# Start of a one-core decoder kernel: first products' squares and splits moved off GpSimd, first weights on ScalarE's queue, fixed split order

## The chip, the cores and the metric

The kernel runs on one core of one Trainium2 chip. The core's engines work side by side, each through its own instructions in order: TensorE (PE; weight loads are shown as PEld), VectorE (DVE), ScalarE (ACT), GpSimd (POOL) and SyncE (SP, which issues transfers). The metric is the device time of one execution in microseconds (us); lower is better.

## The reference, cut to what matters

A two-layer decoder trunk on 256 tokens of 2048 columns in float32. Layer A is gated linear attention, layer B sliding-window attention; each is followed by a squared-ReLU MLP of 8192 columns. The change lies in layer A's first lines:

```python
def rmsnorm(x, g):
    xf = x.astype(jnp.float32)
    y = xf * lax.rsqrt(jnp.mean(xf * xf, axis=-1, keepdims=True) + EPS)
    return (y * g.astype(jnp.float32)).astype(x.dtype)
...
    proj = h @ w_in                      # h = rmsnorm(x, norm_mix[0])
    q, k, v, r, glr = jnp.split(proj, [...], axis=-1)
    log_a = jax.nn.log_sigmoid((glr @ w_g2 + b_g).astype(f32)) / GLA_GATE_TAU
```

## The kernel before

Everything is kept transposed: model columns on the 128 partitions, the 256 tokens along the free dimension. A product over 2048 columns is made in four chunks of 512 (`kq`, or `c`), each of four tiles of 128 (`k`). Every operand is split into a leading half and a correction (float32r), and a product is three matmuls: weights' leading half x operand's leading half, weights' correction x operand's leading half, weights' leading half x operand's correction. A tile `k` of `gemm_sta` is 12 matmuls of 256 columns (4 groups of weight columns x 3), so the first product, `gemm_k(0)`, is 16 such tiles, 192 matmuls.

Three steps make the operands of a tile, and they bear the names used below:

- `split_w`: weights land in `ws`; ScalarE casts them to `wh` (L122), VectorE subtracts to `wl` (L123). The first product loads and splits by single tiles (`step=1`, 256 KB, 128x512); later ones load 1 MB and split by two tiles (128x1024). There are three `ws` buffers and four `wh`/`wl` pairs of two tiles each.
- `scaled`: x times the norm's gain: ScalarE makes the leading half `act` (L226), VectorE the correction (L227). It is 128x256 a tile.
- `load_x` (L271 on) loads a chunk of x in two transfers of 256 KB, calls `scaled` four times and has GpSimd add up x's squares: `ssx` and `sqx`, 128x1024 each (L281, L284, L285); `rstd_x` folds them to `ss` (L295, L296).

The row norm itself (`rstd_of`, `along`) is applied after the products: it is due some half chunks later (`later`, `tick`), and TensorE multiplies `ss` by ones for it after the first half of the next product's first chunk. Between the two products lies `glr`, 16 matmuls of 512 columns into `tp`. `load_gate` loads the gates' weights `wg` (512 KB) on GpSimd's queue and splits them on GpSimd (L334, L335).

A scheduler orders each engine's instructions by program order and priority: transfers and splits of weights come 60 places ahead (`WPRI`), one transfer of x has priority 0 (`XPRI`). All these transfers but `wg` and the gain `go` are issued by SyncE, at most eight in flight: each further one waits until an earlier one has landed.

Before x is there, TensorE runs 11 idle products of ones (`WARM`).

Of the kernel before, what the change touches and what calls it, by code (L numbers as in the profile page):

```python
# [8 lines left out]
F32 = mybir.dt.float32  # L9
# [3 lines left out]
ALU = mybir.AluOpType  # L13
# [25 lines left out]
XPRI = 0  # L39
# [10 lines left out]
def yoco_kernel(ctx: ExitStack, tc: tile.TileContext, x, norms, mlp_w1, mlp_w2, a_w_in, w_glr, w_gate, a_g_o, a_w_o,  # L50
# [18 lines left out]
    # work beside the large products: due so many half pieces of weights later, so that its operands are there  # L69
# [20 lines left out]
    # the norms' gains: a tile of 128 model columns to a column  # L90
    gT = const.tile([P, 5 * KT], F32, name="gT")
    with tc.high_priority(offset=WPRI):
        nc.sync.dma_start(out=gT, in_=norms)
    G_MIX0, G_MIX1, G_MLP0, G_MLP1, G_KV = (gT[:, KT * i:KT * (i + 1)] for i in range(5))
    # the tensor engine's clock rises once the array has been busy for a while: let it be, until x is there
# [9 lines left out]
    def split_w(parts, step=4):  # L105
# [3 lines left out]
        with tc.high_priority(offset=WPRI):  # L109
            for k in range(0, 4, step):  # L110
                ks = slice(k, k + step)
                o = 0
                for ap in parts:
                    n = ap.shape[1]
                    nc.sync.dma_start(out=ws[:, ks, o:o + n],
                                      in_=ap[k * P:(k + step) * P].rearrange("(k p) n -> p k n", p=P))
                    o += n
            n = min(step, 2)
            for k in range(0, 4, n):
                wh, wl = halves[k // 2]  # L120
                js, ks = slice(k % 2, k % 2 + n), slice(k, k + n)
                nc.scalar.copy(out=wh[:, js, :o], in_=ws[:, ks, :o])  # L122
                nc.vector.tensor_sub(out=wl[:, js, :o], in0=ws[:, ks, :o], in1=wh.bitcast(F32)[:, js, :o])  # L123
# [5 lines left out]
    def gemm_mov(src, act, evac, step=4):  # L129
        """out[tok, n] of 512 columns: activations stationary, weights moving. Returns a function of kq."""  # L130
# [23 lines left out]
    def gemm_sta(src, act, evac, widths=(P, P, P, P), step=4):  # L154
        """out^T[n, tok] of up to 512 columns: weights stationary, activations moving. Returns a function of kq."""
# [3 lines left out]
        def run(kq):  # L159
            if kq == 0:  # L160
                accs.extend(bank([P, 2, T], "acc") for _ in range((nf + 1) // 2))
            halves = split_w(src(kq), step)
# [20 lines left out]
    def gemm_wide(src, act, evac, last=False):  # L183
        """As gemm_sta; of each 128 columns the leading product and the sum of the corrections, [2, tok], apart. last:
        the columns end one after the other."""
# [32 lines left out]
    def new_act():  # L218
        """512 of a product's contraction, [128, 4, half of the mantissa, tokens], and the halves alone."""
# [3 lines left out]
    def scaled(act, kt, src, gcol):  # L223
        """Tile kt of an operand chunk: src (x^T, 128 columns of the model) * gain."""
        ah, al, _ = act
        nc.scalar.activation(out=ah[:, kt], in_=src, func=AF.Copy, scale=gcol)  # L226
        nc.vector.scalar_tensor_tensor(out=al[:, kt], in0=src, scalar=gcol, in1=ah.bitcast(F32)[:, kt], op0=ALU.mult,  # L227
                                       op1=ALU.subtract)

    def rsqrt(o, v, src, mul, n):  # L230
        """o = (src * mul + EPS) ** -0.5, [128, n]."""
# [6 lines left out]
    def add_ss(ss, xt, first):  # L238
        """ss += x^2 of two tiles of 128 model columns."""
# [7 lines left out]
    def rstd_of(r, ss):  # L247
        """1 / rms of every token: token on the partition."""
# [6 lines left out]
    def along(rb, r):  # L255
        """The same with the tokens along the free dim, on all partitions."""
# [14 lines left out]
    def load_x(c):  # L271
        """512 columns of the model: as an operand, and their squares' sums."""
        for k in range(0, 4, 2):
            r = c * C + k * P
            with tc.high_priority(offset=XPRI if (c, k) == (0, 2) else WPRI):
                nc.sync.dma_start(out=xt[c][:, k:k + 2], in_=x[r:r + 2 * P].rearrange("(k p) t -> p k t", p=P))
        act0.append(new_act())
        for kt in range(4):
            scaled(act0[c], kt, xt[c][:, kt], G_MIX0[:, c * 4 + kt:c * 4 + kt + 1])
        if c == 0:  # L280
            nc.gpsimd.tensor_mul(out=ssx, in0=xt[c], in1=xt[c])  # L281
        else:
            sq = actp.tile([P, 4, T], F32, name="sqx", tag="act")
            nc.gpsimd.tensor_mul(out=sq, in0=xt[c], in1=xt[c])  # L284
            nc.gpsimd.tensor_add(out=ssx, in0=ssx, in1=sq)  # L285

    ssx = actp.tile([P, 4, T], F32, name="ssx", tag="act")
# [4 lines left out]
    rb4, rbq4 = (a.rearrange("p (o t n) -> p o t n", o=1, t=NT).broadcast_to([P, 2, NT, P]) for a in (rb, rbq))  # L292

    def rstd_x():
        nc.gpsimd.tensor_add(out=ss, in0=ssx[:, :2], in1=ssx[:, 2:])  # L295
        nc.gpsimd.tensor_add(out=ss[:, 0], in0=ss[:, 0], in1=ss[:, 1])  # L296
# [4 lines left out]
    # ================= layer A: gated linear attention =================  # L301
# [4 lines left out]
    # sums over the tokens up to each one: upwards in the first tile, downwards in the second  # L306
# [5 lines left out]
    # of every block of 2s partitions, the half with the earlier tokens  # L312
# [13 lines left out]
    # the gates' product, exact in two passes: glr in quarters of the partitions, see glr()  # L326
# [4 lines left out]
    def load_gate():  # L331
        wg = g2.tile([P, 1024], F32, name="wg", tag="mlev")
        nc.gpsimd.dma_start(out=wg, in_=w_gate)
        nc.gpsimd.tensor_copy(out=wgh, in_=wg)  # L334
        nc.gpsimd.tensor_sub(out=wgl, in0=wg, in1=wgh.bitcast(F32))  # L335
# [555 lines left out]
```

## Time and profile before

| | us |
|---|---|
| Runs, median of 3 | 2107.68 |
| Runs, lowest and highest | 2105.56, 2120.28 |
| Profiled execution, span on the core | 2105.1 |
| TensorE busy in it | 2083.7 (99%) |
| First product's first and last matmul start | 6.17, 48.53 |

The page gives no separate time for the profiled execution; the run nearest to its span is the lowest, 0.5 us above it. The span starts with the first instruction on the core. Busy time of an engine is not progress alone: an instruction that waits inside for a port counts as busy, and so do matmuls at the lower of TensorE's two clocks.

### The profile page before, as it was taken

The page shows a single profiled execution, that of the slowest core. Times are in us where ns is not written, and L with a number is a line of the kernel's source. Part 1 is how long each engine was busy: PE and PEld are TensorE (multiplying, and loading weights), DVE is VectorE, ACT ScalarE, POOL GpSimd, SP SyncE. Part 2 cuts the span into 40 slices and gives each one's busy share as a digit, 9 for nine tenths or more (in the row PEclk, how much of TensorE's full clock was granted, in tenths as well). Part 3 has the DMA queues.
Part 4 walks back from the last instruction along what each step waited for, and adds up shares of the span by engine and source line. Part 5 has one row for each costly group of instructions (what it writes and reads, how often), then busy time and mean ns, then how long its engine had stood idle before and what let it go on. Part 6 is the DMA issues. An engine that isn't in the chain of part 4 may idle for free.

```text
span 2105.1 us, 30277 instructions
## 1 busy us (share of the span) xinstructions
PE 2083.7 (99%) x12290; PEld 1835.0 (87%) x12290; DVE 1282.4 (61%) x1523; ACT 989.4 (47%) x1314; POOL 419.0 (20%) x338
## 2 busy tenths in 40 slices
PE   7999999999999999999999999999999999999999
PEld 6998889988888888888888878988888888888888
DVE  7587444765555555555578576775555655555555
ACT  4645454444434434434455676444434434443442
POOL 6054111322003102201233143232102201200310
PEclk8999999999999999999999999999999999999999
DMA  6544555555565555555655533555556555556564
GB/s 217 178 142 148 174 179 180 180 183 187 192 197 183 198 183 182 198 194 185 196 187 177 184 122 121 179 176 187 198 185 195 182 198 184 188 190 198 182 209 131
DMA packets 195884, 381.40 MB, mean 181 GB/s; under 512 B 6577, under 2 KB 14785, under 8 KB 195745
## 3 DMA queue, kind: packets, MB, share of 16 engines
q1 hardware_dynamic: 195424, 378.60, 54.5%
q8 instruction: 96, 1.57, 0.3%
q0 software_dynamic: 320, 0.87, 0.2%
q14 instruction: 44, 0.35, 0.0%
HBM read 377.35 MB, written 2.10 MB: 180 GB/s over the span
## 4 chain that ended last, share of the span: by engine, by line
PE 93%; DVE 3%; ACT 2%; DMA 1%; issue 1%; POOL 1%; SPq 0%; ACTq 0%; DVEq 0%
PE acc L81 53%; PE ms L81 20%; PE tp L81 18%; DVE wl L123 1%; ACT sc L784 1%; DMA ws<-in_a_w_in_dram 1%; DVE act L227 0%; PE tp L717 0%; ACT wh L122 0%; POOL ss L245 0%; DMA xt<-in_x_dram 0%; DVE xt L584 0%; PE tp L530 0%; DVE st L778 0%; DVE st L780 0%
## 5 line engine op out<-in xcount | busy, mean ns | idle before, releaser
L123 DVE TENSOR_TENSOR wl<-ws,wh 128x1024 fp32r<-128x1024 f32 (+1 forms) x720 | 913.9, 1276 | 634.9 <-ACT wh L122 634.5
L122 ACT CAST wh<-ws 128x1024 fp32r<-128x1024 f32 (+1 forms) x720 | 748.6, 1042 | 841.0 <-PE acc L81 490.1
L81 PE MATMUL acc<-act,wh 128*128 128x512 f32 (+1 forms) x3328 | 955.7, 352 | 12.5 <-DVE act L227 10.9
L81 PE MATMUL acc<-act,wl 128*128 128x256 f32 x2688 | 756.9, 282 | 0.3 <-DVE wl L123 0.2
L81 PEld LDWEIGHTS acc<-act,wh 128*128 128x128 f32 x3328 | 588.5, 190 | 100.7 <-DVE act L227 12.0
L81 PEld LDWEIGHTS acc<-act,wl 128*128 128x128 f32 x2688 | 512.1, 190 | 1.5 <-DVE wl L123 0.8
L81 PE MATMUL tp<-act,wh 128*128 128x512 f32 x1104 | 429.4, 391 | 0.0
L81 PE MATMUL ms<-act,wh 128*128 128x512 f32 x1088 | 425.6, 391 | 0.0
L81 PE MATMUL ms<-act,wl 128*128 128x256 f32 x1088 | 304.7, 280 | 0.0
L81 PE MATMUL tp<-act,wl 128*128 128x256 f32 x1088 | 304.7, 280 | 0.0
L634 POOL TENSOR_TENSOR m<-m,rb 128x512 f32<-128x512 f32 x64 | 82.7, 1292 | 962.4 <-DVE m L629 962.4
L81 PE MATMUL acc<-wh,act 128*128 128x512 f32 x832 | 268.1, 396 | 0.0
L81 PEld LDWEIGHTS tp<-act,wh 128*128 128x128 f32 x1104 | 206.5, 187 | 45.5
L81 PEld LDWEIGHTS ms<-act,wh 128*128 128x128 f32 x1088 | 203.5, 187 | 45.0
L81 PEld LDWEIGHTS tp<-act,wl 128*128 128x128 f32 x1088 | 205.6, 189 | 0.0
L81 PEld LDWEIGHTS ms<-act,wl 128*128 128x128 f32 x1088 | 205.6, 189 | 0.0
L81 PEld LDWEIGHTS acc<-wh,act 128*128 128x128 f32 x832 | 155.7, 188 | 32.7 <-issue 1.0
L81 PE MATMUL acc<-wl,act 128*128 128x512 f32 x416 | 162.2, 390 | 0.0
L637 POOL TENSOR_TENSOR act<-m,act 128x512 fp32r<-128x512 f32 x64 | 99.7, 1558 | 93.3 <-ACT act L636 93.3
L635 DVE SCALAR_TENSOR_TENSOR m<-m 128x512 f32<-128x512 f32 x64 | 44.3, 692 | 102.8 <-POOL m L634 102.8
L636 ACT CAST act<-m 128x512 fp32r<-128x512 f32 x64 | 39.8, 622 | 120.1 <-DVE m L635 120.1
L81 PEld LDWEIGHTS acc<-wl,act 128*128 128x128 f32 x416 | 78.2, 188 | 16.6 <-issue 1.4
(185 smaller groups left out, 1060.2 us busy)
## 6 DMA issues: line engine op xcount, KB each, us to landing
ws<-in_mlp_w_dram SPq DMA_DIRECT2D x256, 1024.0 KB, 5.0
ws<-in_a_w_in_dram SPq DMA_DIRECT2D x44, 1024.0 KB, 5.0
ws<-in_a_w_o_dram SPq DMA_DIRECT2D x16, 1024.0 KB, 4.9
ws<-in_b_w_q_dram SPq DMA_DIRECT2D x16, 1024.0 KB, 4.9
ws<-in_b_w_o_dram SPq DMA_DIRECT2D x16, 1024.0 KB, 5.0
ws<-in_a_w_in_dram SPq DMA_DIRECT2D x16, 256.0 KB, 5.8
xt<-in_x_dram SPq DMA_DIRECT2D x8, 256.0 KB, 5.6
ws<-in_kv_w_k_dram SPq DMA_DIRECT2D x4, 512.0 KB, 3.9
```

The costliest lines, as they stand in the source:

```text
L81: nc.tensor.matmul(o, lhsT=l, rhs=r, start=start, stop=stop, **kw)
L122: nc.scalar.copy(out=wh[:, js, :o], in_=ws[:, ks, :o])
L123: nc.vector.tensor_sub(out=wl[:, js, :o], in0=ws[:, ks, :o], in1=wh.bitcast(F32)[:, js, :o])
L634: nc.gpsimd.tensor_mul(out=m, in0=m, in1=rb2)
L635: nc.vector.scalar_tensor_tensor(out=m2, in0=m, scalar=0.0, in1=m, op0=ALU.max, op1=ALU.mult)
L636: nc.scalar.copy(out=ah[:, bs], in_=m2)
L637: nc.gpsimd.tensor_sub(out=al[:, bs], in0=m2, in1=ah.bitcast(F32)[:, bs])
L784: nc.scalar.activation(out=sc[:, h], in_=sc[:, h], func=AF.Exp, bias=nmx[:, h:h + 1], scale=f[:, h:h + 1], accum_out=su[:, h:h + 1])
```

## The change

- GpSimd no longer squares and adds x: ScalarE squares the four chunks (128x1024, two to a tile of the new `sqx`), VectorE adds them (`sum_x`: 128x2048, 128x1024, 128x512, 128x256). They are due two to five half chunks after the first product's last chunk is handed out.
- The gates' weights are split on ScalarE and VectorE instead of GpSimd, due three half chunks later.
- The norms' gains `gT` and the first chunk's four weight transfers are issued by ScalarE; SyncE starts with x. The x transfer that had priority 0 has 60 like the others.
- In the first chunk an order is enforced (`issue_after`): operand tiles 0 and 1, weights 0 and 1, operand tiles 2 and 3, weights 2 and 3.
- Docstrings and comments were removed.

```diff
-        nc.sync.dma_start(out=gT, in_=norms)
+        nc.scalar.dma_start(out=gT, in_=norms)
...
-    def split_w(parts, step=4):
+    def split_w(parts, step=4, queue=nc.sync, between=None):
...
-                    nc.sync.dma_start(out=ws[:, ks, o:o + n],
-                                      in_=ap[k * P:(k + step) * P].rearrange("(k p) n -> p k n", p=P))
+                    queue.dma_start(out=ws[:, ks, o:o + n],
+                                    in_=ap[k * P:(k + step) * P].rearrange("(k p) n -> p k n", p=P))
...
-                nc.scalar.copy(out=wh[:, js, :o], in_=ws[:, ks, :o])
-                nc.vector.tensor_sub(out=wl[:, js, :o], in0=ws[:, ks, :o], in1=wh.bitcast(F32)[:, js, :o])
+                with ExitStack() as order:
+                    if between:
+                        for ins in between(k):
+                            order.enter_context(tc.issue_after(ins.ins))
+                    h = nc.scalar.copy(out=wh[:, js, :o], in_=ws[:, ks, :o])
+                    l = nc.vector.tensor_sub(out=wl[:, js, :o], in0=ws[:, ks, :o], in1=wh.bitcast(F32)[:, js, :o])
+                if between:
+                    last[:] = h, l
...
-            halves = split_w(src(kq), step)
+            halves = split_w(src(kq), step, *(() if kq else first))
...
-            with tc.high_priority(offset=XPRI if (c, k) == (0, 2) else WPRI):
+            with tc.high_priority(offset=WPRI):
...
-        for kt in range(4):
-            scaled(act0[c], kt, xt[c][:, kt], G_MIX0[:, c * 4 + kt:c * 4 + kt + 1])
-        if c == 0:
-            nc.gpsimd.tensor_mul(out=ssx, in0=xt[c], in1=xt[c])
-        else:
-            sq = actp.tile([P, 4, T], F32, name="sqx", tag="act")
-            nc.gpsimd.tensor_mul(out=sq, in0=xt[c], in1=xt[c])
-            nc.gpsimd.tensor_add(out=ssx, in0=ssx, in1=sq)
+        if c:
+            for kt in range(4):
+                scaled_x(c, kt)
...
+    def scaled_x0(k):
+        if k % 2 == 0:
+            with ExitStack() as order:
+                for ins in last:
+                    order.enter_context(tc.issue_after(ins.ins))
+                scaled_x(0, k)
+                last[:] = scaled_x(0, k + 1)
+        return last
...
+    def square_x(c):
+        if c % 2 == 0:
+            sqx.append(actp.tile([P, 2, 4, T], F32, name="sqx", tag="act"))
+        nc.scalar.activation(out=sqx[c // 2][:, c % 2], in_=xt[c], func=AF.Square)
+
+    def sum_x():
+        a, b = sqx
+        nc.vector.tensor_add(out=a, in0=a, in1=b)
+        nc.vector.tensor_add(out=a[:, 0], in0=a[:, 0], in1=a[:, 1])
+        nc.vector.tensor_add(out=ss, in0=a[:, 0, :2], in1=a[:, 0, 2:])
+        nc.vector.tensor_add(out=ss[:, 0], in0=ss[:, 0], in1=ss[:, 1])
 
     def rstd_x():
-        nc.gpsimd.tensor_add(out=ss, in0=ssx[:, :2], in1=ssx[:, 2:])
-        nc.gpsimd.tensor_add(out=ss[:, 0], in0=ss[:, 0], in1=ss[:, 1])
+        for c in range(NC4):
+            later(2 + c // 2, lambda c=c: square_x(c))
+        later(5, sum_x)
...
-        nc.gpsimd.tensor_copy(out=wgh, in_=wg)
-        nc.gpsimd.tensor_sub(out=wgl, in0=wg, in1=wgh.bitcast(F32))
+        nc.scalar.copy(out=wgh, in_=wg)
+        nc.vector.tensor_sub(out=wgl, in0=wg, in1=wgh.bitcast(F32))
...
-    run = gemm_k(0, step=1)
+    run = gemm_k(0, step=1, first=(nc.scalar, scaled_x0))
...
-    load_gate()
+    later(3, load_gate)
```

ScalarE's first instructions, from the program's start. Before (SyncE issued the transfers then):

```order
L887 UNCONDITIONAL_BRANCH
L100 ACT_TABLE_LOAD
L100 COPY warm<-ones 128x1
L226 ACTIVATE act<-xt,gT 128x256 x2
L122 CAST wh<-ws 128x512 x4
L226 ACTIVATE act<-xt,gT 128x256 x2
L122 CAST wh<-ws 128x512 x2
L226 ACTIVATE act<-xt,gT 128x256
L122 CAST wh<-ws 128x512
```

And now:

```order
L92 DMA gT<-in_norms_dram 128x80
L114 DMA ws<-in_a_w_in_dram 128x512 x4
L231 ACT_TABLE_LOAD
L231 ACTIVATE act<-xt,gT 128x256 x2
L125 CAST wh<-ws 128x512 x2
L231 ACTIVATE act<-xt,gT 128x256 x2
L99 COPY warm<-ones 128x1
L125 CAST wh<-ws 128x512 x6
L231 ACTIVATE act<-xt,gT 128x256 x4
L125 CAST wh<-ws 128x512 x4
```

The transfers stand ahead of the table load, the first chunk alternates by pairs, and the second chunk's four casts (the last four of the six) stand ahead of its four operand tiles.

GpSimd's instructions behind the masks that it builds at the start. Before:

```order
L321 AFFINE_SELECT mask_161<-mask_161 128x64 x2
L281 TENSOR_TENSOR ssx<-xt 128x1024
L284 TENSOR_TENSOR sqx<-xt 128x1024
L333 DMA wg<-in_w_gate_dram 128x1024
L285 TENSOR_TENSOR ssx<-ssx,sqx 128x1024
L284 TENSOR_TENSOR sqx<-xt 128x1024
L285 TENSOR_TENSOR ssx<-ssx,sqx 128x1024
L334 CAST wgh<-wg 128x1024
L335 TENSOR_TENSOR wgl<-wg,wgh 128x1024
L284 TENSOR_TENSOR sqx<-xt 128x1024
L285 TENSOR_TENSOR ssx<-ssx,sqx 128x1024
L295 TENSOR_TENSOR ss<-ssx 128x512
```

And now:

```order
L350 AFFINE_SELECT mask_160<-mask_160 128x64 x2
L401 MEMSET AT 128x1536
L352 AFFINE_SELECT mask_160<-mask_160 128x64 x2
L364 DMA wg<-in_w_gate_dram 128x1024
L239 TENSOR_TENSOR rstd<-rv,mhalf 128x2
```

All eleven instructions on x and on the gates' weights are gone, and the transfer of `wg` stands right behind the masks.

VectorE at the end of the first product and the start of the next (`wh` 128x8x32 is `glr`'s split, 128x1024 are the next product's weights), now:

```order
L126 TENSOR_TENSOR wl<-ws,wh 128x512 x2
L232 SCALAR_TENSOR_TENSOR act<-xt,gT,act 128x256 x2
L377 TENSOR_TENSOR wh<-ws,wh 128x8x32
L319 TENSOR_TENSOR sqx<-sqx 128x2048
L377 TENSOR_TENSOR wh<-ws,wh 128x8x32
L320 TENSOR_TENSOR sqx<-sqx 128x1024
L126 TENSOR_TENSOR wl<-ws,wh 128x1024
L321 TENSOR_TENSOR ss<-sqx 128x512
L366 TENSOR_TENSOR wgl<-wg,wgh 128x1024
L126 TENSOR_TENSOR wl<-ws,wh 128x1024
L322 TENSOR_TENSOR ss<-ss 128x256
```

Before, the two `wh` rows and the `wl` rows followed each other with nothing between them.

## Rows read from the trace of the kernel before

**Rows 1.** Page, busy us of each engine (share of the span), instructions

```profile
PE 2083.7 (99%) x12290; PEld 1835.0 (87%) x12290; DVE 1282.4 (61%) x1523; ACT 989.4 (47%) x1314; POOL 419.0 (20%) x338
```

**Rows 2.** Windows: length, busy us (instructions) PE PEld DVE ACT POOL, clock, DMA, GB/s

```profile
4.00:10.60 6.60, 5.04 (x35) 4.44 (x34) 4.38 (x7) 3.67 (x7) 6.59 (x22) 1.00 0.96 311
10.60:33.20 22.60, 11.37 (x48) 9.99 (x49) 22.38 (x9) 9.86 (x22) 22.12 (x12) 0.60 0.54 203
33.20:48.65 15.45, 15.45 (x122) 15.45 (x121) 10.58 (x21) 5.42 (x7) 0.00 (x0) 0.92 0.77 262
...
22.60:32.50 9.90, 4.70 (x20) 4.21 (x20) 9.90 (x6) 2.11 (x5) 9.58 (x6) 0.50 0.01 2
...
15.00:16.00 1.00, 1.00 (x8) 1.00 (x7) 1.00 (x1) 1.00 (x4) 1.00 (x1) 0.55 1.05 406
...
9.80:14.60 4.80, 0.73 (x4) 0.53 (x4) 4.29 (x3) 4.18 (x9) 4.80 (x6) 1.00 1.06 401
```

**Rows 3.** Waits, first 50 us: who for whom, total us, times, longest

```profile
PE acc L81 <- DVE act L227: 10.9, 4, 3.3
```

**Rows 4.** Timeline of VectorE: start, length, instruction, count, idle before and releaser

```profile
7.46 2.15 DVE L123 TENSOR_TENSOR wl<-ws,wh 128x512 fp32r<-128x512 f32 x3 [0.62 <-ACT wh L122]
10.82 8.55 DVE L227 SCALAR_TENSOR_TENSOR act<-xt,gT,act 128x256 fp32r<-128x256 f32 x2 [0.51 <-ACT act L226]
28.30 2.56 DVE L227 SCALAR_TENSOR_TENSOR act<-xt,gT,act 128x256 fp32r<-128x256 f32 x1
37.73 1.66 DVE L227 SCALAR_TENSOR_TENSOR act<-xt,gT,act 128x256 fp32r<-128x256 f32 x4
39.31 2.48 DVE L123 TENSOR_TENSOR wl<-ws,wh 128x512 fp32r<-128x512 f32 x4
```

**Rows 5.** Timeline of GpSimd

```profile
10.57 1.88 POOL L281 TENSOR_TENSOR ssx<-xt 128x1024 f32<-128x1024 f32 x1
27.91 2.67 POOL L285 TENSOR_TENSOR ssx<-ssx,sqx 128x1024 f32<-128x1024 f32 x1
```

**Rows 6.** Timeline of ScalarE, and one issue of SyncE's queue

```profile
0.79 1.28 ACT L100 ACT_TABLE_LOAD   x1 [0.79 <-PEq L879]
1.23 0.42 SPq L276 DMA_DIRECT2D xt<-in_x_dram  x1
3.95 0.91 ACT L226 ACTIVATE act<-xt,gT 128x256 fp32r<-128x256 f32 x2 [1.67 <-DMA xt<-in_x_dram]
5.50 0.62 ACT L122 CAST wh<-ws 128x512 fp32r<-128x512 f32 x1 [0.64 <-DMA ws<-in_a_w_in_dram]
6.81 2.02 ACT L122 CAST wh<-ws 128x512 fp32r<-128x512 f32 x3 [0.70 <-DMA ws<-in_a_w_in_dram]
10.28 0.91 ACT L226 ACTIVATE act<-xt,gT 128x256 fp32r<-128x256 f32 x2 [1.45 <-DMA xt<-in_x_dram]
33.46 1.14 ACT L122 CAST wh<-ws 128x512 fp32r<-128x512 f32 x2 [8.75 <-PE acc L81]
```

**Rows 7.** Timeline of TensorE's matmuls

```profile
6.17 0.50 PE L81 MATMUL acc<-act,wh 128*128 128x256 f32 x2 [0.52 <-ACT wh L122]
31.51 0.41 PE L81 MATMUL acc<-act,wl 128*128 128x256 f32 x1
32.15 0.41 PE L81 MATMUL acc<-act,wl 128*128 128x256 f32 x1
48.65 3.82 PE L81 MATMUL tp<-act,wh 128*128 128x512 f32 x16
```

**Rows 8.** Chain that ended last, pieces in order of time: start, length, what

```profile
30.92 17.89 PE acc L81 x130
...
110.91 5.75 PE acc L81 x48
```

**Rows 9.** Groups by shape: busy us, mean ns, idle before and releaser

```profile
L123 DVE TENSOR_TENSOR wl<-ws,wh 128x1024 fp32r<-128x1024 f32 x704 | 897.6, 1281 | 633.5 <-ACT wh L122 633.2
L413 ACT ACTIVATE mlev<-mlev 128x1024 f32<-128x1024 f32 x12 | 12.7, 1060 | 28.1 <-DVE mlev L410 28.0
```

More of the change, by code (lines that the diff above doesn't have):

```diff
@@ L38 @@
 LV = 2
-XPRI = 0
 WARM = 11
@@ L152, in gemm_mov, with gemm_sta @@
         return run
-    def gemm_sta(src, act, evac, widths=(P, P, P, P), step=4):
+    def gemm_sta(src, act, evac, widths=(P, P, P, P), step=4, first=(nc.sync,)):
         nf = len(widths)
@@ L225, in scaled @@
         ah, al, _ = act
-        nc.scalar.activation(out=ah[:, kt], in_=src, func=AF.Copy, scale=gcol)
-        nc.vector.scalar_tensor_tensor(out=al[:, kt], in0=src, scalar=gcol, in1=ah.bitcast(F32)[:, kt], op0=ALU.mult,
-                                       op1=ALU.subtract)
+        h = nc.scalar.activation(out=ah[:, kt], in_=src, func=AF.Copy, scale=gcol)
+        l = nc.vector.scalar_tensor_tensor(out=al[:, kt], in0=src, scalar=gcol, in1=ah.bitcast(F32)[:, kt],
+                                           op0=ALU.mult, op1=ALU.subtract)
+        return h, l
     def rsqrt(o, v, src, mul, n):
@@ L274, in load_x, with scaled_x @@
             r = c * C + k * P
-            with tc.high_priority(offset=XPRI if (c, k) == (0, 2) else WPRI):
+            with tc.high_priority(offset=WPRI):
                 nc.sync.dma_start(out=xt[c][:, k:k + 2], in_=x[r:r + 2 * P].rearrange("(k p) t -> p k t", p=P))
         act0.append(new_act())
-        for kt in range(4):
-            scaled(act0[c], kt, xt[c][:, kt], G_MIX0[:, c * 4 + kt:c * 4 + kt + 1])
-        if c == 0:
-            nc.gpsimd.tensor_mul(out=ssx, in0=xt[c], in1=xt[c])
-        else:
-            sq = actp.tile([P, 4, T], F32, name="sqx", tag="act")
-            nc.gpsimd.tensor_mul(out=sq, in0=xt[c], in1=xt[c])
-            nc.gpsimd.tensor_add(out=ssx, in0=ssx, in1=sq)
-    ssx = actp.tile([P, 4, T], F32, name="ssx", tag="act")
+        if c:
+            for kt in range(4):
+                scaled_x(c, kt)
+    def scaled_x(c, kt):
+        return scaled(act0[c], kt, xt[c][:, kt], G_MIX0[:, c * 4 + kt:c * 4 + kt + 1])
+    def scaled_x0(k):
[6 more added lines that the diff above has]
+        return last
+    last = []
     ss = new_ss()
@@ L292, in yoco_kernel @@
     rb4, rbq4 = (a.rearrange("p (o t n) -> p o t n", o=1, t=NT).broadcast_to([P, 2, NT, P]) for a in (rb, rbq))
+    sqx = []
+    def square_x(c):
[8 more added lines that the diff above has]
+        nc.vector.tensor_add(out=ss[:, 0], in0=ss[:, 0], in1=ss[:, 1])
     def rstd_x():
-        nc.gpsimd.tensor_add(out=ss, in0=ssx[:, :2], in1=ssx[:, 2:])
-        nc.gpsimd.tensor_add(out=ss[:, 0], in0=ss[:, 0], in1=ss[:, 1])
+        for c in range(NC4):
+            later(2 + c // 2, lambda c=c: square_x(c))
+        later(5, sum_x)
         later(7, lambda: rstd_of(rstd, ss))
@@ L465, in yoco_kernel, with gemm_k @@
     w_in = a_w_in[0]
-    def gemm_k(c, step=4):
+    def gemm_k(c, step=4, first=(nc.sync,)):
         def evac_k(b, acc):
@@ L471, in evac_k @@
             later(7 if c == 0 else 1, scale)
-        return gemm_sta(piece(w_in, 1024 + c * C), act0, evac_k, step=step)
+        return gemm_sta(piece(w_in, 1024 + c * C), act0, evac_k, step=step, first=first)
     def gemm_q(c):
```

## The prediction

> **What bounds the kernel now.** I read the page first: TensorE is busy for 2083.7 us of the 2105.1 [rows 1], so only the 21.4 us of its idle time, and stretches in which it is busy but slow, can be won. The windows then show where both lie. From 10.60 to 33.20 us TensorE is busy for half of the time and its granted clock is 0.60 on the mean; from 33.20 to the first product's end at 48.65 it never stops [rows 2]. The waits say whom it waited for: 10.9 us in four waits for the operand's correction, which VectorE makes [rows 3].
>
> Why was VectorE late? The timeline of VectorE shows the same instruction at two prices. An operand's correction takes 8.55 us for two at 10.82 and 2.56 us at 28.30, but 1.66 us for four (0.42 each) at 37.73; a weights' correction of 128x512 takes 0.62 each at 39.31 and 0.72 each at 7.46 [rows 4]. What is there between 10.6 and 33.2 and at neither other time is GpSimd's arithmetic on 128x1024: it starts at 10.57, fills 22.12 us of the stretch to 33.20 and is empty after it [rows 2, 5], and VectorE's instruction from 28.30 ends at 30.86, 0.28 us after GpSimd's ends at 30.58 [rows 4, 5]. Transfers are no explanation: from 22.60 to 32.50 they move 2 GB/s, and VectorE is as slow [rows 2]. In this stretch VectorE got through 9 instructions in 22.38 us [rows 2]; at 0.42 for five operands and 0.62 for four weights they are 4.6. So some 17.8 us were lost there, and TensorE with them.
>
> The lost time can also be read from TensorE alone, and this is the form that I use. At full clock 48 matmuls take 5.75 us [rows 8], so a tile of 12 takes 1.44 and the first product's 16 tiles 23.0. They took from 6.17 to 48.65, 42.5 [rows 7]. **19.4 us is the most that can be won here.**
>
> The Trainium skill has a rule for it: SBUF — State Buffer, section Who interferes with whom, says that a VectorE instruction with two SBUF inputs and a GpSimd instruction that reads SBUF take turns, the second blocked until the first ends. The ends 0.28 us apart agree with it.
>
> **The change, part by part.** GpSimd's eleven instructions go, so VectorE's splits cost 0.42 and 0.62 throughout. GpSimd has only masks left, as before 10.57, where VectorE ran at 0.72 [rows 4, 5]. What is then late? I build the new first product from the landings, ScalarE's order and VectorE's.
>
> *Landings.* ScalarE's waits tell when transfers of 256 KB landed: the first at 3.95, the second at 5.50, the third at 6.81 and the eighth (the x transfer of priority 0) at 10.28 [rows 6], so 0.69 each from the third on; later the rate is 406 GB/s [rows 2], 0.65 each. I keep that series and change the order. x (SyncE) and the first weights (ScalarE) come from two queues; no row shows two at once. One bound: they alternate, and weights 0 to 3 land at 5.5, 7.5, 8.9, 10.3. The other: x goes first, and they land at 8.2, 8.9, 9.6, 10.3. I take the first, since both queues start at the same time. The second chunk's weights then land at 10.9 to 13.5 (`go` takes one place), the third's at 16.8 to 18.7 (`wg`, issued some 4 us earlier than before, takes two), the fourth's at 20.7 to 22.6.
>
> *ScalarE's start.* An issue takes 0.42 on SyncE and the table load 1.28 [rows 6]. Five issues from 0.8 and the load end at about 4.4; if an issue costs ScalarE twice that, at 6.5. Weight 0 lands at 5.5, so this costs nothing in the first case and about 1 us in the second; I take the first.
>
> *First chunk.* ScalarE needs 0.57 a cast [rows 6] and 0.43 an operand. The first cast ends at 6.1 and TensorE starts there, as before. It waits 0.56 for the first weights' correction and 0.56 for weight 1, and ends the chunk at 13.0.
>
> *Second chunk.* In ScalarE's order its four casts stand ahead of its four operands, so the first operand waits for the last landed weight: 13.5, cast to 14.1, operand at 14.5. TensorE is idle from 13.0 to 14.56 (1.56) and waits 0.41 more for the correction on VectorE. This is the new wait that takes part of the gain. It also covers the first chunk: with x first, TensorE starts at 8.8 and ends the chunk at 15.1, and the total moves by 0.2 to 0.9 only.
>
> *Third and fourth.* The second ends at 20.7. The third's last weight lands at 18.7, its first operand is there at 19.8 and its correction at 20.4, 0.3 us in time; the fourth's at 23.3 for 26.5. No wait. End: 13.0 + 1.56 + 0.41 + 12 x 1.44 = 32.25, against 48.65: **16.4 us gained.**
>
> The Trainium skill, DMA: Bandwidth & Descriptors, section Issuing engines are not separate DMA queues, speaks against the transfers' move: queues share the same DMA engines, and only issue time is saved. By it the first weights come no earlier in all, which is what both bounds above assume; the sum by it is the same.
>
> *Squares and gates, moved.* Four squares of 128x1024 and a cast of it on ScalarE, at 1.06 each like an exponential of that size [rows 9], 5.3 us. VectorE: 1.28 for 128x1024 [rows 9], 0.62 for 128x512 [rows 4], so about 2.4, 1.3, 0.6, 0.4 and 1.3 for the gates' weights: 6.0 us. They lie under `glr` and the next product, where ScalarE before waited for TensorE to free buffers, 8.75 us at once at 33.46 [rows 6]. ScalarE is done with the first product at 25.0; squares and `glr`'s casts in their order end at 31.3, before TensorE needs the second cast (34.1). VectorE starts the large sum when the squares are there, 30.2, and ends the last at 39.1, behind the next product's two splits. TensorE needs `ss` after `glr` (3.65) and half a chunk (2.88): 38.8. So 0.3 us of wait. Without the cover all 11.3 us would show; with the next splits 1 us later than I have them, 1.3.
>
> **Sum**: 16.4 - 0.3 = 16.1. The profiled execution's own time is 2105.6 (the span and 0.5 around it), so 2089.5. The median of the runs shown lies 2.1 above that execution, and I carry this over: **2091**.
>
> **Rivals.**
> - *The lower clock returns.* Before, the clock was at its lower level from 15.5 on (0.55 granted from 15 to 16), after a stretch from 9.80 to 14.60 with TensorE busy for 0.73 us; its mean of 0.92 over the 15.45 us from 33.20 puts the rise at about 35.6, 4.7 us into unbroken work from 30.92 [rows 2, 8]. At that level (1.2 of 2.4 GHz) three matmuls take 0.64 [rows 7], a tile 2.56, so 1.12 more each. With the gap of 1.56 and two small waits the clock may fall once: four tiles, 4.5 us, 2095.5. Against it: of those 4.80 us TensorE was idle for 4.1, and the new gap is 1.56 with full work on both sides.
> - *Slower than before, by the same mechanism*: if the clock stayed low to the end of `glr` and on, 15 tiles' worth (16.1 / 1.12) eat the gain, and from there it is slower: half clock from 13 us to beyond 48, 2108 to 2112. The rise 4.7 us into unbroken work speaks against it, since nothing here breaks the work after 14.6.
> - *The new work is in the way*: VectorE's 6.0 us ahead of the next product's splits, or a landing 1 us later than in my series (the third chunk has 0.3 to spare). 2 to 4 us lost: 2094.
> - *The gap closes*: if landings run earlier than before with two queues, only the two waits of the first tile remain, and 18.5 us are won: 2088.6, or 2087 for an execution like the profiled one.
> - *The change doesn't do it*: VectorE is slow for another cause, and 2107 stays. The 2 GB/s row and the equal ends speak against it.
>
> **How the numbers follow.** Forecast (13 to 17.5 us gained, 2090 to 2095) 0.66; the gap closes 0.12; lower clock once 0.10; new work in the way 0.07; no change 0.03; slower 0.02. The range takes in the closed gap in a low run and the lower clock: 2086 to 2098. One per cent, about what a measurement of this kernel can tell from no change (the runs shown span 0.7%), is 21 us, more than the 19.4 that can be won, so faster by over 1% needs a low run as well: 0.10. Slower by over 1% 0.02, within 1% 0.88.
>
> **What the profile would show.** Right: VectorE's operand corrections at 0.47 or less and GpSimd empty from 11 us on; the first `tp` matmul at about 32.3; one gap of TensorE of 1 to 2 us at 13, put down to `act` on ScalarE; clock 1.00 from 14 on; ScalarE's squares near 1.06 and no table load beside them. Wrong: a granted clock of 0.50 after 13 us; waits of the casts for landings in the third chunk; TensorE waiting for `ss` for over 1 us; the first matmul later than 9 us.

## The result, and the profile after

| | before | after |
|---|---|---|
| Median of 13 runs each, us | 2108.58 | 2104.04 |
| Lowest, highest, us | 2105.56, 2121.07 | 2090.57, 2104.47 |
| Profiled execution, us (its span) | 2105.6 (2105.1) | 2092.08 (2090.4) |
| First `tp` matmul (end of the first product), us | 48.65 | 32.81 |

The ratio after to before is 0.9934, with a 95% interval of 0.9908 to 0.9961: faster, by less than 1%. The runs of both kernels fall into groups some 13.5 us apart (the last section tells what differs between them): before around 2107.3 (7 runs) and 2120.6 (6), after around 2090.7 (5) and 2104.3 (8). Like compared with like, the change is worth 16.4 to 16.6 us; the medians lie only 4.5 apart because more runs of after fell into the upper group.

The page of after, busy time of each engine (answers to [rows 1]): TensorE is busy 3.9 us less, at the same 12290 matmuls, and its idle time fell from 21.4 to 10.6 us.

```profile
PE 2079.8 (99%) x12290; PEld 1830.7 (88%) x12290; DVE 1269.4 (61%) x1528; ACT 993.3 (48%) x1319; POOL 396.0 (19%) x327
```

The windows of [rows 2], now after (length, busy us and instructions of PE, PEld, DVE, ACT, POOL, then clock, DMA share, GB/s):

```profile
10.60:33.20 22.60, 21.87 (x176) 21.16 (x175) 17.07 (x30) 19.95 (x34) 0.00 (x0) 1.00 0.91 334
33.20:48.65 15.45, 15.45 (x119) 14.85 (x118) 13.44 (x19) 7.43 (x10) 1.03 (x2) 1.00 0.74 247
```

In the 22.6 us in which VectorE before got through 9 instructions and TensorE through 48 matmuls, there are now 30 and 176. GpSimd is empty there, and the clock is granted in full.

VectorE, GpSimd and ScalarE in after (timelines: start, length, line, instruction, count, idle before and who ended it), against [rows 4 to 6]:

```profile
12.14 3.10 DVE L126 TENSOR_TENSOR wl<-ws,wh 128x512 fp32r<-128x512 f32 x5 [0.99 <-ACT wh L125]
15.15 1.67 DVE L232 SCALAR_TENSOR_TENSOR act<-xt,gT,act 128x256 fp32r<-128x256 f32 x4
30.13 2.29 DVE L319 TENSOR_TENSOR sqx<-sqx 128x2048 f32<-128x2048 f32 x1 [1.48 <-ACT sqx L314]
37.82 0.42 DVE L322 TENSOR_TENSOR ss<-ss 128x256 f32<-128x256 f32 x1
...
9.81 0.56 POOL L364 DMA_DIRECT2D wg<-in_w_gate_dram  x1
41.00 0.73 POOL L239 TENSOR_TENSOR rstd<-rv,mhalf 128x2 f32<-128x2 f32 x1 [30.63 <-DVE rv L238]
...
4.14 1.28 ACT L231 ACT_TABLE_LOAD   x1 [4.14 <-DMA gT<-in_norms_dram]
8.24 0.62 ACT L125 CAST wh<-ws 128x512 fp32r<-128x512 f32 x1 [1.39 <-DMA ws<-in_a_w_in_dram]
11.48 2.77 ACT L125 CAST wh<-ws 128x512 fp32r<-128x512 f32 x5 [1.21 <-DMA ws<-in_a_w_in_dram]
14.16 1.70 ACT L231 ACTIVATE act<-xt,gT 128x256 fp32r<-128x256 f32 x4
16.98 2.48 ACT L125 CAST wh<-ws 128x512 fp32r<-128x512 f32 x4 [1.11 <-DMA ws<-in_a_w_in_dram]
25.25 2.00 ACT L314 ACTIVATE sqx<-xt 128x1024 f32<-128x1024 f32 x2
```

Four corrections cost 1.67 us, five weights' corrections 3.10: 0.42 and 0.62 each, the price they had before outside GpSimd's stretch. Two rows say what is late now: the casts at 8.24 and 11.48 waited for weights to land, and the second chunk's operands start only at 14.16, behind its casts.

The chain that ended last, its first pieces (start, length, what), and TensorE's two stops of over 0.2 us behind the first chunk:

```profile
0.80 2.96 DMA gT<-in_norms_dram
...
3.77 7.68 DMA ws<-in_a_w_in_dram
...
11.48 0.63 ACT wh L125
...
15.69 17.29 PE acc L80 x142
```

```profile
6.90 0.50 PE L80 MATMUL acc<-act,wh 128*128 128x256 f32 x2 [0.64 <-ACT wh L125]
...
14.72 0.38 PE L80 MATMUL acc<-act,wh 128*128 128x256 f32 x1 [0.26 <-ACT act L231]
15.69 0.50 PE L80 MATMUL acc<-act,wh 128*128 128x256 f32 x2 [0.47 <-DVE act L232]
32.81 3.82 PE L80 MATMUL tp<-act,wh 128*128 128x512 f32 x16
...
39.34 0.50 PE L80 MATMUL ms<-ones,ss 128*128 128x1 f32 x4
```

The fourth weight transfer was issued only at 3.77, when `gT` had landed, and landed at 11.45; its cast follows at 11.48. From 15.69 on TensorE never stops: the rest of the product is 142 matmuls in 17.29 us.

### The profile page after: what moved, and what is told of

Read it like the earlier page. It is cut to its first block, busy times and chain, and to the rows that moved or that the text cites. A ratio compares the mean times of both kernels' runs of the same rounds, so it can differ in the third digit from the quotient of the medians.

```text
span 2090.4 us, 30272 instructions
## 1 busy us (share of the span) xinstructions
PE 2079.8 (99%) x12290; PEld 1830.7 (88%) x12290; DVE 1269.4 (61%) x1528; ACT 993.3 (48%) x1319; POOL 396.0 (19%) x327
## 4 chain that ended last, share of the span: by engine, by line
PE 93%; DVE 3%; ACT 2%; issue 1%; DMA 1%; POOL 1%; ACTq 0%; DVEq 0%
PE acc L80 54%; PE ms L80 20%; PE tp L80 18%; ACT sc L815 1%; DVE wl L126 1%; ACT wh L125 0%; PE tp L748 0%; DMA ws<-in_a_w_in_dram 0%; DVE st L809 0%; DVE st L811 0%; PE tp L561 0%; DVE po L837 0%; DVE pv L837 0%; DVE act L232 0%; DVE qhl L779 0%
## 5 line engine op out<-in xcount | busy, mean ns | idle before, releaser
L80 PEld LDWEIGHTS acc<-wl,act 128*128 128x128 f32 x416 | 78.2, 188 | 16.6 <-issue 1.4
```

The source lines that it names most:

```text
L80: nc.tensor.matmul(o, lhsT=l, rhs=r, start=start, stop=stop, **kw)
```

## The experiments

The theory: GpSimd's work on 128x1024 stood in VectorE's way, and taking it off GpSimd is the gain. The first rival: the earlier weights and the fixed order are the gain. All comparisons below go by the first `tp` matmul, that is the end of the first product (before 48.65, after 32.81), which the groups of runs don't touch; the expectations call it the first transpose. Times stand beside it. Each kernel's first product is read from one profiled execution. How far two executions of one kernel lie apart is shown by the changed kernel run again, unaltered (the last of these experiments): there the first product ended at 32.25, 0.56 earlier. A difference of half a microsecond between two kernels therefore tells nothing.

**Squares back on GpSimd** (the rest as changed):

```diff
+        if c == 0:
+            nc.gpsimd.tensor_mul(out=ssx, in0=xt[c], in1=xt[c])
+        else:
+            sq = actp.tile([P, 4, T], F32, name="sqx", tag="act")
+            nc.gpsimd.tensor_mul(out=sq, in0=xt[c], in1=xt[c])
+            nc.gpsimd.tensor_add(out=ssx, in0=ssx, in1=sq)
...
-        for c in range(NC4):
-            later(2 + c // 2, lambda c=c: square_x(c))
-        later(5, sum_x)
+        nc.gpsimd.tensor_add(out=ss, in0=ssx[:, :2], in1=ssx[:, 2:])
+        nc.gpsimd.tensor_add(out=ss[:, 0], in0=ss[:, 0], in1=ss[:, 1])
```

> The changed kernel with x's squares and their sums back on GpSimd, where they stood before; the gate weights' split, the queues and the fixed order stay as changed. The theory (VectorE is slowed by GpSimd's two-input work beside it): the squares fill GpSimd from about 10.5 to about 29 us, VectorE's operand corrections there take 1 us and more instead of 0.42, and the first transpose on TensorE, which follows the first product, comes at 43 to 47 us (32.8 in the changed kernel, 48.65 before). The rival (the earlier weights and the fixed order bring the gain): corrections stay slow or not, but the first transpose stays at 33 to 36 us.

Measured: first `tp` at 49.30, time 2108.05 us, ratio to before 0.9988 (0.9961 to 1.0015). VectorE's groups from 10.6 to 30 us (busy us, mean ns, idle before):

```profile
L126 DVE TENSOR_TENSOR wl<-ws,wh 128x512 fp32r<-128x512 f32 x7 | 16.6, 2433 | 1.5 <-ACT wh L125 1.5
L232 DVE SCALAR_TENSOR_TENSOR act<-xt,gT,act 128x256 fp32r<-128x256 f32 x2 | 4.6, 2352 | 0.0
```

2.4 us for what costs 0.62 and 0.42 without GpSimd. The whole gain is gone, and more than I expected (49.3, not 43 to 47). The clock was lower too: its mean was below 1.00 from 10 to 35 us, last in the window below. What of the excess is the clock's, no run tells apart.

```profile
30.00:35.00 5.00, 4.32 (x23) 4.32 (x24) 5.00 (x12) 0.00 (x0) 0.00 (x0) 0.66 0.60 187
```

With the squares still on GpSimd, the queue, the order and the gates' move are worth nothing.

**The move alone** (the kernel before with this part of the change, as in its diff; queues and order as before):

```diff
-        nc.gpsimd.tensor_copy(out=wgh, in_=wg)
-        nc.gpsimd.tensor_sub(out=wgl, in0=wg, in1=wgh.bitcast(F32))
+        nc.scalar.copy(out=wgh, in_=wg)
+        nc.vector.tensor_sub(out=wgl, in0=wg, in1=wgh.bitcast(F32))
...
+        for c in range(NC4):
+            later(2 + c // 2, lambda c=c: square_x(c))
+        later(5, sum_x)
```

> The kernel before with one part of the change alone: squares and gate cast to ScalarE, sums and gate rest to VectorE, all of them later; queues and order of the first chunk as before. The theory: nearly the whole gain, the first transpose at 32.5 to 36 us (48.65 before, 32.8 with the whole change), the time of the kernel 13 to 16 us below the kernel before. The rival (the parts are needed together): the first transpose at 40 us or later.

Measured: first `tp` at 32.66, time 2090.42 us, ratio 0.990 (0.986 to 0.994). All of the gain, without the other two parts: 32.66 lies between the two executions of the changed kernel (32.81 and 32.25). It comes by another path: TensorE starts earlier, at 5.92, and stops longer before the operands of the first chunk's third tile:

```profile
12.16 0.39 PE L81 MATMUL acc<-act,wh 128*128 128x256 f32 x1 [2.26 <-ACT act L226]
```

**One queue** (after with `gT` and the first weights back on SyncE):

```diff
-        nc.scalar.dma_start(out=gT, in_=norms)
+        nc.sync.dma_start(out=gT, in_=norms)
-    run = gemm_k(0, step=1, first=(nc.scalar, scaled_x0))
+    run = gemm_k(0, step=1, first=(nc.sync, scaled_x0))
```

> The changed kernel with the gains and the first chunk's weights back on SyncE's queue; everything else as changed. The theory: the weights come at most some 1.5 us later than on a queue of their own, TensorE starts at 6 to 8 us, and the first transpose stays at 32 to 35 us, so the queue is worth 1 us or less either way. The rival (weights arriving earlier is what shortens the first product): the first transpose at 40 us or later.

Measured: TensorE starts at 8.16, first `tp` at 33.28, time 2091.27 us, ratio 0.990 (0.986 to 0.993). That is 0.47 us later than after and 1.03 later than its second execution, so by these executions the queue is worth 0.5 to 1.0 us of the first product, about what the theory has, and hardly clear of the scatter. (The start is a little later than the 6 to 8 us expected.)

**No fixed order** (after, the first chunk's splits in the scheduler's order):

```diff
-        if c:
+        if True:
             for kt in range(4):
                 scaled_x(c, kt)
-    run = gemm_k(0, step=1, first=(nc.scalar, scaled_x0))
+    run = gemm_k(0, step=1, first=(nc.scalar,))
```

> The changed kernel without the fixed order of the first chunk's splits: the four casts stand ahead of the four operands on ScalarE again. The theory: the fixed order only moves waits within the first chunk, whose end hangs on its last weights (landed at 11.5 us); the first matmul comes up to 2 us later, the first transpose at 32.5 to 34.5 us. The rival (the order is what frees the first product): the first transpose at 40 us or later.

Measured: first `tp` at 37.01, time 2094.67 us, ratio 0.992 (0.989 to 0.995). That lies between the two expectations, 4.2 us worse than after. I had expected a start up to 2 us later; it was 4.7. ScalarE's timeline shows why: the fourth cast waits for the fourth weight, and all four operands wait behind it.

```profile
10.55 0.62 ACT L125 CAST wh<-ws 128x512 fp32r<-128x512 f32 x1 [0.78 <-DMA ws<-in_a_w_in_dram]
11.07 1.70 ACT L231 ACTIVATE act<-xt,gT 128x256 fp32r<-128x256 f32 x4
```

```profile
6.30:11.60 5.30, 0.00 (x0) 0.00 (x0) 2.42 (x5) 2.38 (x6) 3.23 (x7) 0.84 1.02 377
11.63:16.86 5.23, 5.23 (x25) 5.23 (x25) 5.23 (x12) 4.82 (x11) 0.00 (x0) 0.51 1.05 401
```

These are windows of the same kernel: TensorE has no matmul for 5.3 us, and the next two tiles run at a granted clock of 0.51, the lower level, and take 5.23 us for 2.9. So the fixed order is not the gain, but it repairs what the other edits at the start break: without either, in the move alone, the first product ended at 32.66. These edits are the move to ScalarE's queue and the new priority of one x transfer; in the free order no run has one without the other, so which of them does the harm is not shown. Together with the order they are worth nothing on balance.

**What on GpSimd is in the way?** Three kernels: after, with work on GpSimd behind the masks that nothing reads, from about 12 us on: memsets of 128x2048, copies, or products of 128x1024.

```diff
+    dm = actp.tile([P, 2, 4 * T], F32, name="dm", tag="act")
+    nc.gpsimd.memset(dm, 0.5)
+    for _ in range(9):                                  # 9 memsets,
+        nc.gpsimd.memset(dm, 0.5)
+    for _ in range(11):                                 # or 11 copies,
+        nc.gpsimd.tensor_copy(out=dm[:, 1], in_=dm[:, 0])
+    for _ in range(9):                                  # or 9 products
+        nc.gpsimd.tensor_mul(out=dm[:, 1], in0=dm[:, 0], in1=dm[:, 0])
     run = gemm_k(0, step=1, first=(nc.scalar, scaled_x0))
```

> The changed kernel with ten memsets of 128x2048 on GpSimd behind the masks, which nothing reads: GpSimd is busy from about 10.4 to 28 us as before the change, but only writes. If any work on GpSimd slows VectorE: corrections (0.42 us in the changed kernel) take 1 us and more, the first transpose comes at 43 us or later. If only work that reads two operands does: corrections stay under 0.5 us, the first transpose at 32 to 34 us.

> The changed kernel with a memset and eleven copies of 128x1024 on GpSimd behind the masks, which nothing reads: one operand in, one out, about 1.5 us each by the copy of the gate weights before, so busy from 10.4 to about 28 us. If GpSimd's reading as such slows VectorE: corrections over 0.8 us, the first transpose at 40 us or later. If it takes two operands: corrections under 0.5 us, the first transpose at 32 to 34 us. Between the two: 35 to 40 us.

> The changed kernel with a memset and nine products of 128x1024 on GpSimd behind the masks, which nothing reads and which wait for nothing: two operands in, one out, about 1.9 us each by the squares before, so busy from 10.4 to about 29 us. The theory (two-input work of GpSimd slows VectorE, by itself and without any data in common): corrections of 1 us and more, the first transpose at 43 to 50 us. The rival (it was the shared data of x, or waits between the engines): the first transpose at 32 to 35 us.

Measured: first `tp` at 32.46, 40.47 and 45.21. (Their times, one run each, are 2089.78, 2111.68 and 2116.25 us; the latter two hold a long stretch of the slower matmuls of the last section.) A window of each, exactly over the added work, memsets, copies and products in this order:

```profile
12.32:29.10 16.78, 16.04 (x131) 15.63 (x130) 12.81 (x25) 15.60 (x28) 16.32 (x10) 1.00 1.02 369
```

```profile
12.44:26.85 14.41, 8.08 (x46) 7.67 (x45) 14.39 (x11) 9.17 (x20) 13.79 (x11) 0.76 0.92 326
```

```profile
11.75:31.26 19.51, 9.76 (x57) 9.15 (x56) 19.41 (x9) 9.49 (x21) 18.88 (x9) 0.74 0.72 256
```

The fourth bracket is VectorE, the sixth GpSimd. GpSimd is full in all three. Beside memsets VectorE does 25 instructions in 12.81 us, and the first product ends as in after; beside 11 copies it does 11, beside 9 products 9: **one VectorE instruction for each of GpSimd's.** VectorE's groups in the window with the copies and in that with the products show the price:

```profile
L126 DVE TENSOR_TENSOR wl<-ws,wh 128x512 fp32r<-128x512 f32 x7 | 10.3, 1529 | 1.4 <-ACT wh L125 1.4
L232 DVE SCALAR_TENSOR_TENSOR act<-xt,gT,act 128x256 fp32r<-128x256 f32 x4 | 4.8, 1252 | 0.0
```

```profile
L126 DVE TENSOR_TENSOR wl<-ws,wh 128x512 fp32r<-128x512 f32 x5 | 11.6, 2375 | 0.2 <-ACT wh L125 0.2
L232 DVE SCALAR_TENSOR_TENSOR act<-xt,gT,act 128x256 fp32r<-128x256 f32 x4 | 8.2, 2108 | 0.0
```

Beside a copy a correction costs 1.25 us, beside a product 2.11, instead of 0.42. That is what one of GpSimd's takes in the same windows (13.79 us for 11 copies, 18.88 for 9 products, so 1.25 and 2.10): it pays for GpSimd's instruction. So my guess that it takes two operands on GpSimd was wrong: one that is read is enough, writing alone does not count. The data have nothing in common with VectorE's, and nothing waits for them, so the rival of shared data or waits falls. The Trainium skill says the same (SBUF — State Buffer, section Who interferes with whom): a VectorE instruction with two SBUF inputs contends with a GpSimd instruction that reads SBUF, and not with one that only writes it. These three windows agree. All of VectorE's instructions here have two inputs, so how one with a single input fares no run here shows.

**A better order.** TensorE's stops that end at 14.72 and 15.69 come from the second chunk's casts ahead of its operands. Pairs in all chunks:

```diff
-            halves = split_w(src(kq), step, *(() if kq else first))
+            halves = split_w(src(kq), step, *((nc.sync,) + first[1:] if kq else first))
...
-        if c:
-            for kt in range(4):
-                scaled_x(c, kt)
...
+        c = len(act0) - 1
...
-                scaled_x(0, k)
-                last[:] = scaled_x(0, k + 1)
+                scaled_x(c, k)
+                last[:] = scaled_x(c, k + 1)
```

> The changed kernel with the operands ahead of the casts by pairs in the second to fourth chunk too; queues as in the changed kernel. By its tile starts (12 products each, 1.44 us unstalled) the fifth and sixth tile lost 0.66 and 0.81 us there, behind the second chunk's casts. The theory: these 1.47 us go, the first product ends at 31.2 to 31.8 us instead of 32.8, and the span follows by as much. The rival (the last weights of the first chunk and the second chunk's data set the pace, whatever the order): 32.4 to 33 us.

Measured: first `tp` at 31.32, so 1.49 earlier than after, within the range of the theory, but in part by luck. TensorE starts at 6.39 here instead of 6.90: `gT` released ScalarE at 3.63 instead of 4.14, and nothing in this edit touches that (the changed kernel run again started at 6.43). The rest, 0.98 us, is the first product itself, which became shorter (24.93 us from its first matmul to the first `tp`, against 25.91). The expectation also names the wrong tiles: the 0.66 us went between the starts of the fourth tile and the fifth (0.26 of them is the stop before the fifth), and the 0.81 between those of the fifth and the sixth. The window from the fourth tile to the end of the product shows no stop:

```profile
12.60:31.32 18.72, 18.72 (x159) 18.72 (x158) 13.69 (x25) 16.24 (x29) 0.00 (x0) 1.00 0.99 362
```

Its time, 2116.42 us, was measured where the kernel before took 2133.79, ratio 0.9919 (0.9905 to 0.9934). Two variants of it tried to start earlier as well, by issuing the gains elsewhere, so that ScalarE's fourth weight issue waits for no landing. On GpSimd's queue:

```diff
-        nc.scalar.dma_start(out=gT, in_=norms)
+        nc.gpsimd.dma_start(out=gT, in_=norms)
```

> The changed kernel with two things more: the operands ahead of the casts by pairs in the second to fourth chunk too (as in the first), and the gains on GpSimd's queue, so that ScalarE's weight issues don't wait for them. The theory: TensorE's stop at 14 to 17 us (about 1.2 us in sum) and the late start (6.9 instead of 6.1 us) go: the first transpose at 30.5 to 31.8 us instead of 32.8, and the time 1 to 2 us below the changed kernel. The rival (the second chunk's weights, landed at 11.9 to 13.6 us, and its x at 8.8 to 9.8 are what TensorE waits for): 32.3 to 33 us, no difference.

Measured: first matmul at 8.50, first `tp` at 33.43, median 2091.16 us, ratio 0.9925 (0.9896 to 0.9953). On SyncE's queue, ahead of x:

```diff
-        nc.scalar.dma_start(out=gT, in_=norms)
+        nc.sync.dma_start(out=gT, in_=norms)
```

> The same, and the gains back ahead of x on SyncE's queue, so that ScalarE's fourth weight issue waits for no landing. The theory: the first product starts at 6.1 to 6.6 us instead of 6.9, its last first-chunk weights land up to 1 us earlier, and it ends at 30.5 to 31.5 us. The rival: x comes 0.5 us later by the issue ahead of it, and first weights and x share the same transfer engines, so nothing is won over the run beside it: within 0.4 us of that.

Measured: first matmul at 9.00, first `tp` at 34.06, time 2118.51 us, 2.1 more than the version beside it. Neither theory nor rival was right: both are worse. ScalarE's timelines, first with the gains on GpSimd's queue, then on SyncE's:

```profile
5.04 1.28 ACT L231 ACT_TABLE_LOAD   x1 [5.04 <-DMA xt<-in_x_dram]
7.03 0.91 ACT L231 ACTIVATE act<-xt,gT 128x256 fp32r<-128x256 f32 x2 [0.71 <-DMA gT<-in_norms_dram]
```

```profile
6.24 1.28 ACT L231 ACT_TABLE_LOAD   x1 [6.24 <-DMA xt<-in_x_dram]
```

On GpSimd's queue the gains themselves come late. On SyncE's, x holds ScalarE until 6.24, where in after `gT` released it at 4.14 with x already there. x is issued 0.44 later there, so some 1.7 us of the 2.1 come from elsewhere. Two transfers were moved ahead there: the fourth weight, issued without a wait, and one weight of the second chunk, which SyncE issued at 2.21 (in after its first at 3.94). That they take x's place is what I conclude; no run shows it by itself. What is shown: the wait for `gT`, which looks like a loss in the chain of after, cost less than these two ways of avoiding it.

**Both side by side**, the changed kernel and the version with pairs in all chunks on one chip, 12 runs each:

> The changed kernel once more, unaltered, beside the version with pairs in all chunks on the same chip, for a direct comparison. Expected: the first product ends at 32.5 to 33 us; the time lies 15 to 17 us below the kernel before wherever both run at the same pace of matmuls.

> The version with operands ahead of casts in all chunks, beside the unaltered changed kernel on the same chip. The theory: its first product ends at 31.2 to 31.5 us and its time lies 1.0 to 1.8 us below the changed kernel's at the same pace of matmuls. The rival (the time of later stages moves by more than this from run to run, or they give it back): a difference under 0.7 us.

Measured: first `tp` at 32.25 and 31.20, from 6.43 and 6.82 on, so the first product took 25.82 us and, with the pairs, 24.38. The first row of the changed kernel's TensorE, its stop before the second chunk, and its first `tp`:

```profile
6.43 0.50 PE L80 MATMUL acc<-act,wh 128*128 128x256 f32 x2 [0.59 <-ACT wh L125]
14.41 0.38 PE L80 MATMUL acc<-act,wh 128*128 128x256 f32 x1 [0.80 <-ACT act L231]
32.25 1.09 PE L80 MATMUL tp<-act,wh 128*128 128x512 f32 x4
```

The changed kernel ended it 0.25 us ahead of the 32.5 to 33 that I expected of it. The runs fell into three groups: before around 2107.8, 2120.4 and 2133.7; changed 2090.4, 2105.4 and 2117.5; pairs 2089.5, 2103.6 and 2116.3. Group by group the change is worth 17.4, 15.0 and 16.2 us, and the pairs a further 0.9, 1.9 and 1.2 (ratio to before 0.994 (0.990 to 0.998) and 0.992 (0.988 to 0.996)). The theory of 1.0 to 1.8 us about fits, and the rival (under 0.7) does not; but the lowest group holds one run of each, and the runs within the middle group lie up to 2 us apart.

## Why the prediction was right, and where not

**The cause** was right: GpSimd's work on 128x1024 made VectorE late, and VectorE made TensorE late. Undoing the squares' move alone takes the gain away, making the moves alone brings all of it, and foreign work on GpSimd brings the loss back. The equal ends and the 2 GB/s of [rows 2, 4, 5], on which it rested, pointed the right way; the experiments show it. What the prediction did not know is the price: one of GpSimd's instructions for each of VectorE's, and a copy is enough.

**The first product** was forecast to end at 32.25 and ended at 32.81: 15.84 us won instead of 16.4. The difference of 0.56 is made of four terms that were each off:
- First matmul at 6.90 instead of 6.1: +0.80. My sum had ScalarE through its five issues at 4.4 with the table load; the fourth weight issue waited for `gT`'s landing, so the load began at 4.14 and ended at 5.42, between the two bounds given (4.4 and 6.5). What I missed is that the limit of eight transfers in flight, which I had named for SyncE, covers ScalarE's issues too: `gT`, three weights and four of x make eight.
- First chunk 7.56 us (6.90 to 14.72 less the stop of 0.26) instead of 6.9: +0.66. Weights 1 and 3 were cast at 8.24 and 11.48 as they landed, against 7.5 and 10.3 in my series.
- Stop for the second chunk's operands 0.26 instead of 1.56: -1.30. It is the same wait, `act` on ScalarE behind four casts, but the first chunk ended later and covered most of it.
- The fifth tile then lost 0.81 instead of 0.41 to the correction: +0.40.

The same kernel run again shows how much of this is scatter, and luck: its terms were off by +0.33 (start 6.43), +0.28, -0.76 (stop 0.80) and +0.15, the same way each, and cancelled, so it ended at 32.25 as forecast to the digit. That the end came out so close is errors that cancel, and not four right terms: the later the first chunk ends, the shorter is the stop for the second chunk's operands.

**Third and fourth chunk**: TensorE did not wait, as forecast. ScalarE's casts there did wait for landings, 1.11 us at 16.98, which the prediction names as a sign of being wrong. It was a bad sign: by its own series the third chunk's weights land from 16.8 on, so its casts had to wait, and TensorE, which was still at the second chunk, was not reached by it.

**`ss`**: forecast late by 0.3; it was there at 38.24 (37.82 + 0.42) instead of 39.1, and TensorE, which took it at 39.34, didn't wait. The squares took 1.0 each (2.00 for two), the sums 2.29 and 0.42 against 2.4 and 0.4, and there was no table load beside them. The cover held.

**The queue**: both bounds said that the weights' queue changes the total by less than a microsecond, and with one queue it was 0.47 against after and 1.03 against its second execution. But I took queue and order as one edit and never costed the queue without the order, which was 4.2 us worse.

**The sum**: 15.84 at the end of the first product, of which the profiled execution shows 14.7 at the end of the span. The missing 1.15 us went between 1078 and 1136 us. The move-alone kernel runs the same program there, 0.15 us earlier, without this loss. Windows from 1060 to 1160, first after, then the move alone:

```profile
1060.00:1160.00 100.00, 98.40 (x525) 83.34 (x524) 80.61 (x122) 52.70 (x74) 28.55 (x19) 1.00 0.58 192
```

```profile
1060.00:1160.00 100.00, 98.36 (x532) 84.20 (x530) 81.08 (x121) 53.45 (x76) 29.47 (x19) 1.00 0.56 192
```

TensorE is as busy and gets 7 matmuls less done. Its matmuls of 512 columns were slower between 1078 and 1136, again first after, then the move alone:

```profile
L80 PE MATMUL acc<-act,wh 128*128 128x512 f32 x64 | 22.7, 399 | 0.0
```

```profile
L81 PE MATMUL acc<-act,wh 128*128 128x512 f32 x64 | 22.2, 391 | 0.0
```

That is the slower pace of the last section and no work of the change.

**The median**: 2104.04 lies 6 us above the range of 2086 to 2098, though the profiled execution (2092.08) and the lower group (2090.7, forecast 2091) lie in it. The step that failed is the last one, "the median of the runs shown lies 2.1 above that execution, and I carry this over": of three runs of before one stood at 2120.28, and I used that scatter for the chance of faster by over 1% but not for the range. A case in which the median falls into the upper group belonged there, with 2104. (The sum has a slip besides: 2089.5 and 2.1 are 2091.6, and I wrote 2091.)

**The rivals**: the lower clock did not return in after (1.00 throughout), but the price set on it was real: in the kernel without the fixed order a stop of 5.3 us was followed by two tiles at the lower level. The gap did not close of itself; the pairs closed it, and the first product then ended at 31.2 to 31.3, so 17.3 to 17.5 us were won and not the 18.5 of that case.

## What to carry to other kernels

Where VectorE's instructions cost several times what the same shape costs elsewhere, look at what GpSimd does beside them: here each VectorE instruction with two inputs paid for one of GpSimd's that reads SBUF, one for one, and for a memset it did not. Move such work to an engine that waits at that time (here ScalarE, 5 us under the next product), and test the parts of a change one by one: two of the three here (the queue and the order) brought nothing together, and one of these cost 4 us without the other. Run the unaltered kernel twice before half a microsecond of one trace is read as an effect. A wait in the chain is not yet a loss: here two ways of taking one away made the start 1.6 to 2.6 us later.

## What the runs showed of the hardware

**Two paces of the matmul at a granted clock of 1.00.** One profiled execution of the version with the gains on GpSimd's queue lasted 13.5 us longer than the move alone, though the two were less than 0.8 us apart from 20 to 1400 us. The windows 400 to 700 and 1700 to 2080, first of the move alone, then of that execution, then of the version with pairs in all chunks where the kernel before took 2133.79:

```profile
400.00:700.00 300.00, 299.95 (x1730) 263.91 (x1729) 175.99 (x203) 133.16 (x161) 53.45 (x38) 1.00 0.56 190
...
1700.00:2080.00 380.00, 380.00 (x2195) 335.06 (x2194) 215.21 (x256) 161.17 (x184) 45.40 (x32) 1.00 0.57 187
```

```profile
400.00:700.00 300.00, 299.95 (x1730) 263.94 (x1730) 176.01 (x204) 133.86 (x161) 53.47 (x38) 1.00 0.58 190
...
1700.00:2080.00 380.00, 380.00 (x2153) 329.47 (x2152) 213.12 (x254) 159.85 (x183) 45.25 (x32) 1.00 0.59 190
```

```profile
400.00:700.00 300.00, 299.96 (x1701) 259.94 (x1700) 173.77 (x201) 130.93 (x159) 53.29 (x38) 1.00 0.56 186
...
1700.00:2080.00 380.00, 380.00 (x2153) 329.43 (x2152) 213.52 (x255) 159.08 (x183) 45.24 (x32) 1.00 0.57 188
```

TensorE is busy throughout in all six and gets through 1.7 to 1.9% fewer matmuls in three of them. The matmuls of 512 columns take 399 instead of 391 ns there (first the move alone, then the slower execution, groups from 1700 to 2000 us):

```profile
L81 PE MATMUL acc<-act,wh 128*128 128x512 f32 x419 | 145.6, 391 | 0.0
```

```profile
L80 PE MATMUL acc<-act,wh 128*128 128x512 f32 x425 | 150.5, 399 | 0.0
```

VectorE's splits keep their price (1253 and 1254 ns each from 1700 to 2080) and so do ScalarE's casts (1054 and 1050 from 1500 to 2000), so of these three it is TensorE alone. In the profiles at hand the upper group has the second of the two long MLP stretches (from about 1400 us) at the slower pace, and the third group, 26 us above the lowest, has the first (from about 450) too. What sets the pace stays open: none of these runs was made to tell it, and the profile's granted clock reads 1.00 at either. For comparing kernels it means: look at which group each run is in before a median is read.
